# First mixer of a hybrid decoder step: the two heads of a pair in turns, the samples' inverse beside the last pair's, sample taps and channel sums on other engines, a fixed order at the end

## The chip, the cores and the metric

The kernel runs on one core of one Trainium2 chip. The metric is the device time of one execution in microseconds (us), the median of several runs. A core has five engines, each of which works off its own queue of instructions strictly in order: TensorE (PE in the rows; its weight loads are PEld), VectorE (DVE), ScalarE (ACT), GpSimd (POOL) and SyncE (SP), which here only issues DMAs. PE writes its products to banks of PSUM; the other engines take them from there.

## What is computed

One inference step of a two-layer trunk, on 512 new tokens of a prompt and on 8 samples of 4 tokens each, with the same weights. Layer 0 is the mixer that the change touches and a feed-forward block; layer 1 is a state-space mixer and a feed-forward block. The mixer, cut to what matters:

```python
def mixer_ab(x, conv_st, shift_st, wkv_st, w_in, conv_w, conv_b, ln_g, ln_b, mu, ...):
    p = x @ w_in                                   # 1024 -> 2816 channels
    pa, pb = p[..., :2 * D_A], p[..., 2 * D_A:]    # D_A = 512
    u = pa[..., :D_A] * jax.nn.sigmoid(pa[..., D_A:])
    ext = jnp.concatenate([conv_st, u], axis=1)
    ya = jax.nn.silu(layer_norm(causal_depthwise(ext, conv_w, conv_b), ln_g, ln_b))   # 31 taps
    q = pb + (prev - pb) * mu
    r, k, v, wl, al, gl = jnp.split(q, SPLIT_B, axis=-1)
    ...
    def step(s, inp):                              # 8 heads of 64, a 64 x 64 state each
        r_t, k_t, v_t, d_t, kk_t, a_t = inp
        sa = jnp.einsum('bhvk,bhk->bhv', s, -kk_t)
        s = s * d_t + sa[..., None] * (kk_t * a_t) + v_t[..., None] * k_t
        return s, jnp.einsum('bhvk,bhk->bhv', s, r_t)
    y, new_wkv = wkv_recurrence(r, k, v, decay, kk, a, wkv_st)
    y = group_norm(y) * lnx_g + lnx_b + bonus
    return jnp.concatenate([ya, y * g], axis=-1) @ w_out, ...
```

The layer norm of `ya` runs over the 512 channels. The recurrence is computed in chunks of 64 tokens, for which a triangular matrix per chunk and head has to be inverted.

## The kernel before

**Layout.** Channels lie on the 128 partitions, tokens along the free side: 544 tokens, 512 of the prompt and 32 of the samples, taken in two halves of 256 and 288. Weights come by DMA as 128 x 512 tiles (`wraw`); ACT makes a high part `whi` and DVE, for some POOL, a low part `wlo`. Inputs are split likewise (`xh`, `xl`). Every product with weights is three matmuls (`xh,whi`, `xl,whi`, `xh,wlo`), for each of 8 input tiles and two halves: 48 for an output tile of 128 channels. These are the matmuls of L201, called gemms here. The product with `w_in` has 22 output tiles. That with `w_out` has 8 output tiles, in two parts: part 0 takes the 4 tiles of channels of the convolution (24 gemms an output tile), the other part the 4 of the recurrence.

**The convolution.** For each of 4 channel tiles `conv_in` forms `u` (tiles `uext` for the prompt, `usam` for the samples) from its two gemm tiles. The 31 taps are each one DVE instruction on the prompt's sums (`cacc<-uext,cols,cacc`, 128 x 512) and one on the samples' (`cacc<-usam,cols,cacc`, 128 x 32). `conv_end` is the layer norm over all channels and comes when all four tiles have their taps: POOL adds up the four tiles, one matmul of a matrix of ones sums over partitions (L610), DVE subtracts the mean, ACT squares, POOL adds the squares, L622 sums them, then root, reciprocal, scaling and the split for `w_out`.

**The recurrence.** The 8 heads go as 4 pairs, numbered 0 to 3, one pair on 128 partitions. Of a pair:
- `pair_in` makes r, k, v, the decay and so on from the gemms.
- `pair_front` is `wkv_front` and `wkv_solve`. `wkv_front` issues 32 matmuls `ps_wf<-ar,kb` (L737, 64 rows, 128 columns): head 0 first, then head 1, the whole of a head through the one bank `wf` twice; DVE masks the result into `xa` and `xk`. DMAs bring the 16 x 16 diagonal blocks of `xa` through memory (`dx`, `xb`) to one block a partition; `wkv_solve` inverts them in 30 small POOL operations (`stmp`, `mm`); DMAs bring them back (`dm`, `mn`).
- `pair_mid` is `wkv_mid` and `wkv_tail`. It begins with the matmuls `ps_wo<-mn,xa` (L813, tile pz), which need `mn`; further products L821 to L843 complete the inverse, L852 multiplies it in, head 0 and then head 1, each in one bank of `wo`; L871 and L877 form what the scan needs.
- `pair_out` is `wkv_scan` (7 steps one behind the other: L894 on PE, then `st` on DVE), the matmuls L901 for the output, the norm of each head (L686, L706), the gate (L552) and the product `yb`.

The samples have their own path: `sample_front` (with an inverse of 16 blocks, L927 to L938), `sample_mid`, `sample_end`.

**What sets the order.** The stages are Python generators that `weave` advances by priorities while the gemms of `w_in` are emitted; a scheduler then orders each engine's queue. Banks of PSUM are taken by tag: 3 of `mm` for the gemms, 1 `wi`, 1 `wf`, 2 `wo`, 1 `wb`. The last calls of the mixer's first part are

```python
        weave((hi, pair_out(2)), (hi, pair_mid(3)), (md, sample_front()), (lo, conv_taps(3)))
        weave((hi, pair_out(3)), (hi, sample_out()), (0, conv_end()))
```

and the first part of `w_out` is emitted with the second of them.

## Time and profile before

| | |
|---|---|
| time, median of 3 runs | 1540.21 us (1530.88 to 1545.67) |
| the profiled execution | 1539.81 us |
| its span in the trace | 1538.0 us (1.8 us lie around it) |
| first mixer in the span | from 0 to about 441 us |
| PE, DVE, ACT, POOL busy | 1433.1, 1023.0, 603.9, 300.1 us |

The profiled execution lies 0.4 us under the median, so its rows can be read as those of a typical run. The three runs lie 14.8 us apart, about 1% of the time.

The change touches the first 441 us alone. The text speaks of four stages of it: 44 to 264 us, when the gemms of `w_in` run and everything else is woven between them; 264 to 338, from the last of these gemms to the first of `w_out`; 338 to 395, the first part of `w_out` with the last pair and the samples beside it; and 395 to 441, the second part of `w_out` and the norm behind it.

### The profile page before, as it was taken

Reading aid. Unit: us, or ns where it says so; the run is one execution under the profiler, and the core shown is the slowest. Engines: PE = TensorE matmul, PEld = TensorE weight load, DVE = VectorE, ACT = ScalarE, POOL = GpSimd, SP = SyncE. Lnnn points to the kernel's source line nnn. Section 1 sums busy time; section 2 is a strip of 40 time slices with the busy share of each in tenths; the row PEclk is TensorE's granted clock in tenths of the full one; section 3 lists DMA queues with packets and bytes.
Section 4 is the critical chain, followed back from the end, with each engine's and each line's share of the span. In section 5 each row is a group of like instructions: output and inputs, shape, how many; then the busy total and the mean of one; then the engine's idle time right before and its main releaser. Section 6 shows DMA issues by size and latency. Waiting matters only on the chain.

```text
span 1538.0 us, 30946 instructions
## 1 busy us (share of the span) xinstructions
PE 1433.1 (93%) x11952; PEld 1371.2 (89%) x11952; DVE 1023.0 (67%) x2437; ACT 603.9 (39%) x1385; POOL 300.1 (20%) x442
## 2 busy tenths in 40 slices
PE   7999999689879999999999879799989999999996
PEld 6987887468879999999999879799989999999996
DVE  6698796765888988656985557555575555554334
ACT  5444352141354445543222443243454444442222
POOL 1252542531320201001561311003200000000200
PEclk9999999689989999999999989789999999999998
DMA  5222113111214244423675469742212222222321
GB/s 187 73 61 66 45 53 102 21 26 50 83 40 130 87 143 171 153 90 111 201 209 180 163 211 306 229 136 89 81 61 91 88 85 90 90 83 86 93 76 59
DMA packets 131939, 169.13 MB, mean 110 GB/s; under 512 B 46912, under 2 KB 72512, under 8 KB 131536
## 3 DMA queue, kind: packets, MB, share of 16 engines
q1 hardware_dynamic: 107536, 130.47, 27.5%
q10 hardware_dynamic: 20944, 22.53, 4.5%
q0 software_dynamic: 3312, 14.16, 2.6%
q8 instruction: 94, 1.54, 0.4%
q14 instruction: 53, 0.43, 0.1%
HBM read 138.59 MB, written 32.71 MB: 111 GB/s over the span
## 4 chain that ended last, share of the span: by engine, by line
PE 73%; DVE 8%; DMA 7%; POOL 4%; issue 3%; ACT 3%; SPq 1%; ACTq 0%; POOLq 0%; DVEq 0%
PE ps_mm L201 62%; PE ps_wk L201 4%; POOL stmp L179 2%; POOL mm L179 2%; DVE wlo L179 2%; DVE xres L179 1%; DVE xres L176 1%; DMA wraw<-in_w_down 1%; PE ps_wf L737 1%; ACT xres L173 1%; DVE cacc L176 1%; DMA tm<-dt 1%; DMA du<-ue 1%; DMA dk<-s5a 1%; ACT whi L271 1%
## 5 line engine op out<-in xcount | busy, mean ns | idle before, releaser
L201 PE MATMUL ps_mm<-xh,whi 128*128 128x256 f32 (+1 forms) x2016 | 491.0, 298 | 19.4 <-ACT whi L271 6.5
L201 PE MATMUL ps_mm<-xl,whi 128*128 128x256 f32 (+1 forms) x2016 | 491.3, 295 | 5.2 <-DVE xl L176 5.0
L201 PE MATMUL ps_mm<-xh,wlo 128*128 128x256 f32 (+1 forms) x2016 | 490.2, 294 | 0.0
L179 DVE TENSOR_TENSOR wlo<-wraw,whi 128x512 fp32r<-128x512 f32 x342 | 255.4, 749 | 252.0 <-ACT whi L271 251.1
L271 ACT CAST whi<-wraw 128x512 fp32r<-128x512 f32 x372 | 226.1, 611 | 472.2 <-PE ps_mm L201 386.2
L201 PEld LDWEIGHTS ps_mm<-xh,whi 128*128 128x128 f32 x2016 | 354.3, 194 | 26.6 <-ACT whi L271 10.6
L201 PEld LDWEIGHTS ps_mm<-xl,whi 128*128 128x128 f32 x2016 | 356.3, 194 | 10.4 <-DVE xl L176 5.6
L201 PEld LDWEIGHTS ps_mm<-xh,wlo 128*128 128x128 f32 x2016 | 355.4, 193 | 4.3 <-issue 3.5
L201 PE MATMUL ps_mm<-fh,whi 128*128 128x256 f32 (+1 forms) x648 | 145.1, 290 | 0.0
L201 PE MATMUL ps_mm<-fl,whi 128*128 128x256 f32 (+1 forms) x648 | 144.5, 289 | 0.0
L201 PE MATMUL ps_mm<-fh,wlo 128*128 128x256 f32 (+1 forms) x648 | 144.3, 289 | 0.0
L201 PEld LDWEIGHTS ps_mm<-fh,whi 128*128 128x128 f32 x648 | 107.5, 188 | 1.8 <-issue 1.6
L201 PEld LDWEIGHTS ps_mm<-fh,wlo 128*128 128x128 f32 x648 | 107.7, 188 | 0.1
L201 PEld LDWEIGHTS ps_mm<-fl,whi 128*128 128x128 f32 x648 | 107.6, 188 | 0.0
L176 DVE SCALAR_TENSOR_TENSOR c<-ps_mm,cols,c 128x254 f32<-128x254 f32 (+3 forms) x264 | 98.5, 395 | 1.8 <-ACT edge L1195 1.4
L176 DVE SCALAR_TENSOR_TENSOR cacc<-uext,cols,cacc 128x512 f32<-128x512 f32 x120 | 94.3, 786 | 2.8 <-ACT cacc L173 1.5
L179 POOL TENSOR_TENSOR ln_s<-xres 128x256 f32<-128x256 f32 (+1 forms) x8 | 10.8, 1367 | 320.6 <-DVE xres L179 320.6
L179 POOL TENSOR_TENSOR wlo<-wraw,whi 128x512 fp32r<-128x512 f32 x30 | 39.6, 1332 | 150.5 <-ACT whi L271 146.5
L179 DVE TENSOR_TENSOR c<-ps_mm,c 128x256 f32<-128x256 f32 (+1 forms) x88 | 35.8, 437 | 49.2 <-PE ps_mm L201 47.1
L201 PE MATMUL ps_mm<-yl,whi 128*128 128x256 f32 (+1 forms) x240 | 57.7, 296 | 3.4 <-DVE yl L179 3.4
L201 PE MATMUL ps_mm<-yh,whi 128*128 128x256 f32 (+1 forms) x240 | 58.5, 299 | 0.3 <-ACT sg L173 0.3
L201 PE MATMUL ps_mm<-yh,wlo 128*128 128x256 f32 (+1 forms) x240 | 57.9, 296 | 0.0
(382 smaller groups left out, 2084.5 us busy)
## 6 DMA issues: line engine op xcount, KB each, us to landing
wraw<-in_w_up SPq DMA_DIRECT2D x176, 256.0 KB
wraw<-in_w_down SPq DMA_DIRECT2D x80, 256.0 KB
wraw<-in_w_in_ab SPq DMA_DIRECT2D x44, 256.0 KB
ds<-trig SPq DMA_DIRECT2D x8, 768.0 KB
ang<-ds POOLq DMA_DIRECT2D x8, 768.0 KB, 6.0
wraw<-in_w_out_c SPq DMA_DIRECT2D x21, 256.0 KB
wraw<-in_w_out_ab SPq DMA_DIRECT2D x16, 256.0 KB
df<-s5a ACTq DMA_DIRECT2D x8, 512.0 KB
```

What stands on the lines that cost most here:

```text
L173: return self.nc.scalar.activation(out, in_, f, **k)
L176: return self.nc.vector.scalar_tensor_tensor(out, a, s, b, op0, op1)
L179: return (eng or self.nc.vector).tensor_tensor(out, a, b, op=op)
L201: ins = self.nc.tensor.matmul(*a, **k)
L271: self.nc.scalar.copy(hi, src)
L737: nc.tensor.matmul(pa[:, i], lhsT=flat(kb[HS[hd], c // 2, c % 2]), rhs=ar[HS[hd], :, c], start=True, stop=True)
```

## The change

1. `wkv_front`: the two heads alternate, matmul by matmul, each with a bank of its own (`wf` and a bank of `wo`); the four DMAs to `dx` are issued at the end. In `wkv_mid` the matmuls of L852 (now L880) go to two banks, in the order of the blocks, which is four in a row on the same 64 x 64 quarter of PE.
2. The samples' 16 blocks are inverted in the same 30 POOL operations as the 64 of pair 3 (80 partitions); `sample_in` is woven into `pair_front(3)`.
3. The samples' taps: a POOL product of 128 x 496 (`spr<-usam,cols`, all 31 taps of two tokens of each sample, twice a channel tile), a DVE sum over taps, and the bias on ACT. The 120 DVE instructions of `cacc<-usam` go.
4. `conv_end`: four matmuls in a row into one bank sum over channels and partitions (L630, and L641 for the squares), in banks of `mm`; the sums on POOL go.
5. The order at the end: the matmuls L630 stand behind the last scan matmul of pair 2 (`scanned`); the first gemms of `w_out` (output tiles m = 0 and 1) follow; the first matmuls of `pair_mid(3)` (L840, before L813) stand behind the newest of these gemms (`behind`); the other output tiles are woven at low priority with `pair_mid(3)` and `pair_out(3)`.

The core of the diff:

```diff
@@ mm
-        ins = self.nc.tensor.matmul(*a, **k)
+        ins = self.newest = self.nc.tensor.matmul(*a, **k)
@@ conv_in, conv_taps
-            self.act(cs, usam[:, 0:32], AF.Identity, scale=w(0), bias=cb)
+            ws = self.cols[:, o:o + 31].unsqueeze(1).unsqueeze(1).broadcast_to([P, 2, NS, 31])
+            for j in range(0, NJ, 2):
+                pr = gp.tile([P, 512], F32, name="spr", tag="spr", bufs=1)
+                pr = pr[:, 0:2 * NS * 31].rearrange("p (j s t) -> p j s t", s=NS, t=31)
+                win = bass.AP(at.tensor, at.offset + NS * j, [at.ap[0], (NS, 2), (1, NS), (NS, 31)])
+                self.tt(pr, win, ws, ALU.mult, nc.gpsimd)
+                nc.vector.tensor_reduce(cs[:, NS * j:NS * j + 2 * NS].rearrange("p (j s) -> p j s", s=NS), pr,
+                                        mybir.AxisListType.X, ALU.add)
+            self.act(cs, cs, AF.Identity, bias=cb)
             for t in range(1, 31):
                 self.stt(ca, uext[:, t:t + NP], w(t), ca, ALU.mult, ALU.add)
-                self.stt(cs, usam[:, 8 * t:8 * t + 32], w(t), cs, ALU.mult, ALU.add)
@@ pair_front
+            solve = self.wkv_solve(p, [(dx, 8, self.mn), (dxs, 4, self.mns)])
+            for step in (front, front, sample, solve, front, solve, front, solve, front, sample, sample):
+                next(step)
+                yield
@@ conv_end
-                self.tt(s1[:, H], cacc[:, 0, H], cacc[:, 1, H], ALU.add, nc.gpsimd)
-                for i in (2, 3):
-                    self.tt(s1[:, H], s1[:, H], cacc[:, i, H], ALU.add, nc.gpsimd)
-                pm = self.bank([P, 512], "wf")
-                nc.tensor.matmul(pm[:, :n], lhsT=self.con("ones"), rhs=s1[:, H], start=True, stop=True)
+                pm = self.bank([P, 512])
+                for i in range(4):
+                    ins = nc.tensor.matmul(pm[:, :n], lhsT=self.con("ones"), rhs=cacc[:, i, H], start=i == 0, stop=i == 3)
+                    for b in behind:
+                        self.chain([b, ins])
                 for i in range(4):
                     self.stt(cacc[:, i, H], pm[:, :n], -1.0 / 512, cacc[:, i, H], ALU.mult, ALU.add)
-                    if i == 0:
-                        self.act(q[:, H], cacc[:, i, H], AF.Square)
-                    else:
-                        self.act(t[:, H], cacc[:, i, H], AF.Square)
-                        self.tt(q[:, H], q[:, H], t[:, H], ALU.add, nc.gpsimd)
+                    self.act(sqs[i][:, H], cacc[:, i, H], AF.Square)
@@ mixer_ab, the last calls
-        weave((hi, pair_out(2)), (hi, pair_mid(3)), (md, sample_front()), (lo, conv_taps(3)))
-        weave((hi, pair_out(3)), (hi, sample_out()), (0, conv_end()))
+        rest = conv_end(self.scanned)
+        weave((hi, pair_out(2)), (lo, conv_taps(3)), (lo, after(8, islice(rest, 6))))
+        behind = [self.newest]
+        weave((hi, seq(lambda: pair_mid(3, behind), lambda: pair_out(3))), (0, sample_out()), (lo, rest))
@@ wkv_front
-        for hd in range(2):
-            for g in range(2):
-                pa = self.bank([P, 4, 2, 64], "wf")
-                for i in range(4):
-                    c = 4 * g + i
+        for g in range(2):
+            pas = [self.bank([P, 4, 2, 64], t) for t in ("wf", "wo")]
+            for i in range(4):
+                c = 4 * g + i
+                for hd, pa in enumerate(pas):
                     nc.tensor.matmul(pa[:, i], lhsT=flat(kb[HS[hd], c // 2, c % 2]), rhs=ar[HS[hd], :, c], start=True,
                                      stop=True)
@@ wkv_mid
-        for h in range(2):
-            pw = self.bank([P, 4, 2, 64], "wo")
-            for c, c2, cp, j, hd, S, O in all_:
-                if hd == h:
-                    nc.tensor.matmul(pw[S, j].rearrange("p a t -> p (a t)"), lhsT=n64[S, h, cp],
+        pws = [self.bank([P, 4, 2, 64], "wo") for _ in range(2)]
+        for c, c2, cp, j, hd, S, O in all_:
+            nc.tensor.matmul(pws[hd][S, j].rearrange("p a t -> p (a t)"), lhsT=n64[S, hd, cp],
@@ wkv_scan
+            self.scanned[:] = [ins]
```

How the change moves instructions, at three places. On PE near the end of the gemms of `w_in`, the front of pair 3 before: groups of four of L737 into `wf` with gemms (L201) between them.

```order
L201 MATMUL ps_mm<-xl,whi 128x288
L201 MATMUL ps_mm<-xh,wlo 128x288
L737 MATMUL ps_wf<-ar,kb 128x128 x4
L201 MATMUL ps_mm<-xh,whi 128x288
L201 MATMUL ps_mm<-xl,whi 128x288
L201 MATMUL ps_mm<-xh,wlo 128x288
L894 MATMUL ps_wb<-st,gtt 64x64 x2
L528 MATMUL ps_wi<-xres,cons 128x256
L852 MATMUL ps_wo<-R,n_3076 64x128 x11
L737 MATMUL ps_wf<-ar,kb 128x128 x4
```

The same front after, on PE behind the last gemm of `w_in`; L851 and L858 are products of `pair_mid(2)` (before L821 and L828).

```order
L924 MATMUL ps_wb<-st,gtt 64x64 x4
L760 MATMUL ps_wf<-ar,kb 128x128
L760 MATMUL ps_wo<-ar,kb 128x128
L851 MATMUL ps_wo<-z,mn 32x32 x11
L760 MATMUL ps_wf<-ar,kb 128x128
L760 MATMUL ps_wo<-ar,kb 128x128
L760 MATMUL ps_wf<-ar,kb 128x128
L760 MATMUL ps_wo<-ar,kb 128x128
```

The heads alternate between two banks, and the front of pair 3 and most of `pair_mid(2)` no longer stand between gemms.

On PE at the turn to `w_out`, before: `conv_end` (L610, L622), the scan of pair 2 (L894) and `pair_mid(3)` (L843, L852) stand mixed.

```order
L843 MATMUL ps_wo<-n_3604,x 32x32 x14
L894 MATMUL ps_wb<-st,gtt 64x64
L901 MATMUL ps_wi<-qt,st 64x64 x2
L610 MATMUL ps_wf<-xres,cons 128x288
L852 MATMUL ps_wo<-R,n_3604 64x128
L894 MATMUL ps_wb<-st,gtt 64x64 x2
L901 MATMUL ps_wi<-qt,st 64x64 x2
L852 MATMUL ps_wo<-R,n_3604 64x128 x15
L622 MATMUL ps_wf<-xres,cons 128x256
```

There after (L924 is the scan, L969 and L970 the samples' front, L728 a head norm, L207 the gemms):

```order
L969 MATMUL ps_wf<-cons,sv 32x128
L970 MATMUL ps_wf<-cons,skb 64x128
L708 MATMUL ps_wi<-cons,sqt 128x2 x4
L924 MATMUL ps_wb<-st,gtt 64x64 x2
L976 MATMUL ps_wf<-swv,xs 32x64 x8
L924 MATMUL ps_wb<-st,gtt 64x64 x8
L630 MATMUL ps_mm<-cacc,cons 128x256 x4
L630 MATMUL ps_mm<-cacc,cons 128x288 x4
L728 MATMUL ps_wi<-cons,rq_y 64x128 x8
L641 MATMUL ps_mm<-xres,cons 128x256 x4
L641 MATMUL ps_mm<-xres,cons 128x288 x4
```

The scan of pair 2 ends ahead of `conv_end`, and nothing of pair 3 stands here any more: L840 follows 48 gemms of `w_out` further down.

On POOL, what stands ahead of the front of pair 3, before (`kb` is its input):

```order
L531 COPY sv<-v 128x32
L179 TENSOR_TENSOR sar<-xres,pexs 128x32
L179 TENSOR_TENSOR skb<-xres,rps 128x32
L179 TENSOR_TENSOR k<-k,xres 128x544
L179 TENSOR_TENSOR kb<-k,xres 128x4x64 x2
```

and after:

```order
L185 TENSOR_TENSOR sar<-xres,pexs 128x32
L185 TENSOR_TENSOR spr<-usam,cols 128x496
L185 TENSOR_TENSOR skb<-xres,rps 128x32
L185 TENSOR_TENSOR k<-k,xres 128x544
L185 TENSOR_TENSOR spr<-usam,cols 128x496
L185 TENSOR_TENSOR kb<-k,xres 128x4x64 x2
```

The two sample products of the last channel tile, which need the last gemm tile of `w_in`, now stand ahead of `kb` of pair 3.

## Rows read from the trace of the kernel before

**Rows 1.** Busy time by stage: window, length, busy of PE, PEld, DVE, ACT, POOL, PEclk, DMA share, GB/s.

```profile
44.00:264.00 220.00, 210.90 (x2130) 185.49 (x2130) 176.08 (x393) 86.20 (x189) 87.69 (x168) 0.96 0.24 66
264.00:338.00 74.00, 53.52 (x665) 40.34 (x664) 52.19 (x107) 23.23 (x55) 38.55 (x79) 0.74 0.14 30
338.00:395.00 57.00, 55.85 (x559) 46.20 (x560) 36.59 (x101) 12.12 (x32) 7.55 (x6) 0.89 0.16 53
```

**Rows 2.** PE's waits, 40 to 264 us: total, times, longest, in us.

```profile
PE ps_wo L813 <- DMA mn<-dm: 8.5, 4, 3.1
```

**Rows 3.** Timeline of DVE at the start: start, length, last column the wait before.

```profile
19.42 1.71 DVE L176 SCALAR_TENSOR_TENSOR cacc<-usam,cols,cacc 128x32 f32<-128x32 f32 x10
...
21.97 1.01 DVE L176 SCALAR_TENSOR_TENSOR wa<-ps_mm,cols,wa 128x256 f32<-128x256 f32 x3
```

**Rows 4.** Timeline of PE at the start.

```profile
22.50 0.56 PE L201 MATMUL ps_mm<-xh,whi 128*128 128x288 f32 x1 [2.42 <-DVE wa L176]
```

**Rows 5.** Timeline of PE around the last gemm of w_in.

```profile
261.79 1.16 PE L737 MATMUL ps_wf<-ar,kb 64*128 64x128 f32 x8
262.87 0.40 PE L201 MATMUL ps_mm<-xh,whi 128*128 128x288 f32 x1
...
263.24 0.29 PE L201 MATMUL ps_mm<-xh,wlo 128*128 128x288 f32 x1
...
264.36 1.52 PE L852 MATMUL ps_wo<-R,n 64*64 64x128 f32 x22
265.81 0.37 PE L737 MATMUL ps_wf<-ar,kb 64*128 64x128 f32 x1
```

**Rows 6.** PE's groups of instructions, 44 to 264 us.

```profile
L737 PE MATMUL ps_wf<-ar,kb 64*128 64x128 f32 x120 | 18.4, 288 | 0.0
```

**Rows 7.** Chain that ended last, 150 to 190 us: start, time on the chain.

```profile
155.43 0.95 PE ps_wf L756 x27
187.67 0.72 PE ps_wo L828 x18
```

**Rows 8.** Tile cacc, its taps: duration in ns min/median/max, first and last start.

```profile
L176 DVE SCALAR_TENSOR_TENSOR cacc<-usam,cols,cacc x120: 228/244/1353, 16.9 to 266.7; 128x32 f32<-128x32 f32 x120
L176 DVE SCALAR_TENSOR_TENSOR cacc<-uext,cols,cacc x120: 720/748/1819, 67.5 to 302.9; 128x512 f32<-128x512 f32 x120
```

**Rows 9.** Timeline of POOL, the inverse of pair 3.

```profile
276.68 0.67 POOL L179 TENSOR_TENSOR stmp<-xb,mm 64x15 f32<-64x15 f32 x1 [4.67 <-DMA xb<-dx]
...
294.40 0.21 POOL L179 TENSOR_TENSOR stmp<-xb,mm 64x15 f32<-64x15 f32 x1
```

**Rows 10.** Tile sm on POOL.

```profile
L179 POOL TENSOR_TENSOR sm<-swv,cons x2: 1488/1518/1549, 372.4 to 378.0; 128x512 f32<-128x512 f32 x2
```

**Rows 11.** Timeline of DVE, 264 to 338 us.

```profile
264.87 2.10 DVE L176 SCALAR_TENSOR_TENSOR cacc<-usam,cols,cacc 128x32 f32<-128x32 f32 x4
...
302.39 0.28 DVE L176 SCALAR_TENSOR_TENSOR st<-ps_wb,pend,xp 128x64 f32<-128x64 f32 x1 [6.36 <-PE ps_wb L894]
...
302.86 0.74 DVE L176 SCALAR_TENSOR_TENSOR cacc<-uext,cols,cacc 128x512 f32<-128x512 f32 x1
...
305.60 0.69 DVE L179 TENSOR_TENSOR z<-ps_wo,cons 128x512 f32<-128x512 f32 x1
```

**Rows 12.** Timeline of PE, 299 to 340 us.

```profile
301.44 0.58 PE L813 MATMUL ps_wo<-mn,xa 64*64 64x64 f32 x3 [6.91 <-DMA mn<-dm]
...
336.30 1.07 PE L877 MATMUL ps_wo<-xk,wv 128*64 128x64 f32 x16
337.83 0.58 PE L201 MATMUL ps_mm<-xh,whi 128*128 128x256 f32 x1 [0.46 <-ACT xh L271]
```

**Rows 13.** Matmuls of line 610: durations, first and last start.

```profile
L610 PE MATMUL ps_wf<-xres,cons x4: 379/444/483, 317.4 to 320.0; 128*128 128x256 f32 x2, 128*128 128x288 f32 x2
```

**Rows 14.** Chain that ended last, 264 to 445 us.

```profile
371.45 1.05 PE ps_wi L561 x2
...
394.74 6.73 PE ps_mm L201 x40
```

More of the change, by code (lines that the diff above doesn't have):

```diff
@@ L114, in constants, with seq @@
     return [np.concatenate([v[n] for n, _ in names], 1).astype(np.float32) for names in (_CONS, _CONS0)]
+def seq(*gens):
+    for g in gens:
+        yield from g()
 def after(n, gen):
@@ L812, in wkv_mid @@
         for c, c2, cp, j, hd, S, O in all_:
-            nc.tensor.matmul(pz[S, hd, cp], lhsT=xa[S, hd, c], rhs=mn[S, hd, cp, 0], start=True, stop=True)
+            ins = nc.tensor.matmul(pz[S, hd, cp], lhsT=xa[S, hd, c], rhs=mn[S, hd, cp, 0], start=True, stop=True)
+            for b in behind:
+                self.chain([b, ins])
         z = new("z", 64, "s2k", S2)
@@ L898, in wkv_scan @@
         py = self.bank([P, 8, 64], "wi")
[L899 removed]
+        for cs in ((1, 2), (3, 4), (5, 6), (7,)):
             for H in HS:
[L901 removed]
+                for c in cs:
+                    nc.tensor.matmul(py[H, c], lhsT=st[H, c], rhs=qt[H, c % 2, c // 2], start=True, stop=True)
         y = d["y"][:, 64:NP]
```

88 lines of the change are left out of this document (49 added, 39 removed).

## Prediction

> **What bounds the kernel now.** I read the busy time by stage first. While the gemms of `w_in` run (44 to 264 us), PE is busy 210.9 of 220 us at a granted clock of 0.96: PE is the bound, and what is taken from it there is gained [rows 1]. Its waits say what fills most of the rest: 8.5 us for `mn`, the inverse coming back by DMA [rows 2]. Between the last gemm of `w_in` and the first of `w_out` (264 to 338) PE is busy 53.5 of 74 us at 0.74: here it waits for others. DVE works through the taps of the last channel tile until 303.6, with a hole of 6.4 us, in which it waits for a scan matmul (L894) [rows 11]; PE at that time stands at the first matmul of `pair_mid(3)`, which waits 6.9 us for `mn` [rows 12]. Queues being in order, the scan of pair 2, DVE and so `conv_end` wait for the inverse of pair 3. L610 comes at 317.4 [rows 13], the first gemm of `w_out` at 337.8 [rows 12]. From 338 to 395 PE is full again, 55.9 of 57 us [rows 1], and the second part of `w_out` starts at 394.7 [rows 14]. That start is the landmark of my sum: behind it the program is the same, instruction for instruction, and bound by PE. The profiled execution took 1539.8, so a gain of g us at the landmark gives 1539.8 less g; it lies 0.4 under the median, which I neglect.
>
> **Start.** Before the first evacuation `wa`, DVE does at least ten sample taps in 1.7 us, and PE waits 2.4 us for it [rows 3, 4]. The taps go. I take 2.5 us off; between 0, if the input transfers set the pace, and 4, if the gemms after the wait come at a better clock.
>
> **Heads in turns.** Before, 8 matmuls L737 take from 261.79 to 262.87, 135 ns each [rows 5]. They use one half of PE's rows at a time. In turns, with a bank for each head, two can run at once. The nearest rows for overlapping small matmuls are L756 and L828, 64 columns, at 35 and 40 ns [rows 7]; for 128 columns L852 takes 1.45 us for 22, 66 ns [rows 5]. So the price halves, and for 96 matmuls of pairs 0 to 2 (120 stand in the window, 24 of them pair 3's [rows 6]) that is 96 x 0.069 = 6.6; I take 7 with pair 3's. Bounds: 0, if halves of rows do not overlap, and 7. The wait for `mn` should fall from 8.5 to about 6.5, since the front is shorter while DMAs and POOL's inverse stay; 2 us, give or take 4.
>
> The Trainium skill ("TensorEngine Tiling (Array Packing)", Gotcha 1) says that different row tiles cannot use the same PSUM bank at once, which would be the reason for 135 ns in one bank and bears out the halving. The same page (Key Properties) says that different tiles run in parallel, and so, read strictly, four L880 in a row on one tile would not; rows of L756 and L828, which are issued four in a row on a tile, stand at 35 and 40 ns against it.
>
> **What moves past the last gemm of `w_in`.** The 24 front matmuls of pair 3 in the window (3.2 us) and the products L821 to L843 of `pair_mid(2)` (128 at about 40 ns, 5.1 us), with single ones of L706 and L552: some 10 us that no longer stand between gemms but beside DVE's taps. The last gemm, at 263.2 [rows 5], so ends about 2.5 + 7 + 2 + 10 = 21.5 earlier, near 242.
>
> **From there to `conv_end`.** DVE sets this. Before it took from 264.9 to 303.6, 38.7 us. Less the hole (6.4, whose cause, pz of pair 3 in front of the scan, is moved away) and four sample taps (2.1 [rows 11]) it is 30.2. To it come evacuations of the front of pair 3 and of `pair_mid(2)` (about 6 us at 0.4 to 0.7 each), two sums over taps at the price of a 128 x 512 tile (0.69 [rows 11]), and a wait: POOL's two sample products now stand ahead of `kb`, at up to 1.5 us each [rows 10], so the front of pair 3 cannot start until some 8 us behind the last gemm, and DVE's evacuation of it stands between the taps: 2 to 4 us. Together 40; bounds 34 and 46. The scan of pair 2 now follows the taps, and L630 it. Nearest price: before, last tap 303.6 to L610 317.4, 13.8 us, in which five of the scan steps and the samples' front stood; I take 14, bounds 9 and 20. L630 is thus at 242 + 40 + 14 = 296, where L610 stood at 317.4.
>
> On POOL the first small operation of the inverse takes 0.67 us beside the taps and the same one 0.21 when DVE is done with most of them [rows 9]. The Trainium skill ("GPSIMD Engine Reference", Specifications) gives the reason, SBUF interfaces shared with VectorE where its instruction has two SBUF inputs; the trace agrees. By it the sample products, 8 of them, might cost DVE's taps too; their median of 748 ns [rows 8] already contains POOL's work, and I add nothing.
>
> **`conv_end`.** Before, L610 to the first gemm took 20.4 us. POOL's sums and their handoffs to ACT go (about 5), eight matmuls of sums more than before are added twice, at 0.4 each [rows 13], part of them beside the evacuations: 15, bounds 12 and 20. First gemm at 311 (before 337.8). 48 gemms for m = 0 and 1 at 0.13 to 0.17: 7.5. So the first matmul of `pair_mid(3)`, gated behind them, runs at 318.5, where it ran at 301.4. Its `mn` is there: the front ends near 265, before 266.9, and the inverse of 80 rows takes the same 30 operations.
>
> **The last pair.** Here the gain is given back. Before, from pz to the second part of `w_out` took 394.7 - 301.4 = 93.3 us: 36 to the end of L877 [rows 12], in part queued behind the samples' front and `conv_end`; then the scan between gemms, to L561 at 371.5; then the head norm and gate, 23.3 to 394.7 [rows 14]. Now `pair_mid(3)` has priority over the remaining 144 gemms, and its scan comes when they are gone, at 14 us or less, in place of 34. 36 less some 7 for what is no longer queued ahead, 14 and 23 make 73; gemms no longer between the norm's steps take 7 off: 66. PE's own work there, the 55.9 us of the stage [rows 1] less 7.5 for m = 0 and 1, lies below that. Landmark 318.5 + 66 = 384.5, 10.2 earlier: **1529.6**.
>
> **Rivals.**
> *The chain of pair 3 gives all back.* With 76 us in place of 66 the landmark is where it was: 1540. For it: scan and norms then run with PE empty and its clock low, which the 0.74 of the stage with waits shows [rows 1]. Against it: 93.3 contained the samples' front and `conv_end`.
> *Slower.* The gate puts pz behind `conv_end`, and everything of pair 3 behind pz. If that chain still takes what it took, 93.3, because each of its steps waits for the step before and not for a free engine, the landmark is 411.8, the time 1557. It decides from 76 us on.
> *Better.* If DVE takes 36 in place of 40 and the scan 10 in place of 14, and the tail takes 60, because the remaining gemms fill the gaps of `pair_mid(3)`, the gain is 10 + 4 + 4 + 6 = 24: 1516. For it: holes of 20 us in the second stage are what the fixed order fills. Against: DVE has little idle time there.
> *It does not do what it says.* If the halves of rows don't overlap, 7 are missing: 1537.
>
> If L880 does run alone on its tile, as the page's rule has it, it takes 135 in place of 66 ns, 128 x 0.069 = 8.8 us more, of which three quarters stand in stages bound by PE: 1536. I give this rival 3 in 100, as the rows speak against it.
>
> **How the numbers follow.** Forecast 0.40 (own range 1521 to 1538), all given back 0.19, slower 0.09, better 0.23, not as said 0.09 with L880. About 1% (15.4 us) is what a measurement of this kernel can tell from no change, since three runs of it lie that far apart. Faster by over 1% (below 1524.8): the better case, and a third of the forecast's, 0.36. Slower by over 1%: 0.08. Within: 0.56. The range leaves out the lower third of the better case and most of the slower one: 1508 to 1547.
>
> **What would show it.** Matmuls of the front in pairs at 60 to 70 ns, and no slower L880; DVE without `cacc<-usam`; the last gemm of `w_in` at 238 to 246; no hole in the taps before the scan; L630 near 296; first gemm near 311; L840 directly behind m = 1, without a wait for `mn`; the second part of `w_out` near 384. What would make it wrong: POOL's products slow enough (above 1.5 us) to hold the front in every pair; a scan of pair 2 of more than 20 us; the wait for `mn` growing with the POOL work; or a stage behind the mixer that starts at another clock.

## The result, and the profile after

The median is 1547.0 us over 20 runs (1535.0 to 1556.7), against 1538.5 for the kernel before (20 runs, 1524.6 to 1545.7): ratio 1.0067, 95% interval 1.0045 to 1.0088. The change makes the kernel 0.7% slower; 1529.6 was predicted, and the measured time lies at the upper edge of the range.

The profiled execution of the changed kernel took 1535.0 us, the lowest of its 20, so its span (1533.2 us) says nothing about the median: the unchanged program behind the landmark took 1129.6 us in it, 1143.3 in the profiled execution of before, and 1130.1 to 1150.5 in the traces of the experiments. What can be compared is the landmark itself, the start of the second part of `w_out`: 403.6 us, before 394.7 [rows 14], so 8.8 later. That the medians differ by as much is chance, since 13.7 us less lie behind it. Run 13 below, whose only edit is that SyncE issues four loads, shows an ordinary execution (1546.7 us of span): there the landmark is 412.3. Each landmark is that of one execution, so a few us between two of them show little by themselves.

Busy time by stage after, cut where the last gemm of `w_in`, the first of `w_out` and the landmark stand (columns as in [rows 1]):

```profile
44.00:247.00 203.00, 191.99 (x1923) 172.18 (x1922) 154.92 (x296) 82.53 (x183) 86.43 (x165) 0.95 0.23 61
247.00:320.00 73.00, 55.10 (x549) 40.60 (x547) 54.03 (x110) 20.86 (x46) 20.97 (x41) 0.72 0.21 54
320.00:404.00 84.00, 73.85 (x886) 61.58 (x887) 46.22 (x128) 18.91 (x51) 7.30 (x7) 0.79 0.11 37
404.00:450.00 46.00, 32.38 (x220) 31.76 (x219) 36.71 (x81) 16.49 (x35) 18.76 (x20) 0.83 0.26 85
```

The first stage is 17 us shorter and the second as long as before [rows 1]; the third takes 84 us in place of 57, at a granted clock of 0.79 in place of 0.89. The gain of the first stage is real and is spent in the third.

The timeline of PE after: last gemm of `w_in`; sums of `conv_end` (L630); first gemm of `w_out`; pz of pair 3; the head norm of pair 3; the landmark.

```profile
246.75 0.29 PE L207 MATMUL ps_mm<-xh,wlo 128*128 128x288 f32 x1
...
305.35 6.79 PE L630 MATMUL ps_mm<-cacc,cons 128*128 128x256 f32 x16
...
320.13 0.39 PE L207 MATMUL ps_mm<-xh,whi 128*128 128x256 f32 x1 [2.25 <-ACT xh L277]
...
332.70 0.68 PE L840 MATMUL ps_wo<-mn,xa 64*64 64x64 f32 x12
...
392.08 1.87 PE L708 MATMUL ps_wi<-cons,sqt 128*128 128x2 f32 x8 [1.36 <-ACT sqt L179]
...
397.90 1.98 PE L728 MATMUL ps_wi<-cons,rq_y 128*64 128x128 f32 x16 [0.46 <-DVE rq_y L182]
400.73 2.08 PE L581 MATMUL ps_wi<-gl,g 128*128 128x512 f32 x2 [0.85 <-DVE y L182]
403.58 0.82 PE L207 MATMUL ps_mm<-xh,whi 128*128 128x256 f32 x2 [0.78 <-DVE yb L185]
```

Against [rows 5, 12, 13]: 16.5 us earlier, 12.1 earlier (L610 then), 17.7 earlier, then pz 31.3 later and the landmark 8.8 later.

Where the second stage stays long is seen on DVE, POOL and PE. Timeline of DVE after: the last taps, the two halves of `xp` of pair 2, with which its `pair_mid` ends, and the first step of its scan.

```profile
277.93 8.62 DVE L182 SCALAR_TENSOR_TENSOR cacc<-uext,cols,cacc 128x512 f32<-128x512 f32 x11
288.48 0.42 DVE L185 TENSOR_TENSOR xp<-ps_wo,pend 128x256 f32<-128x256 f32 x1 [1.94 <-PE ps_wo L906]
...
295.06 0.42 DVE L185 TENSOR_TENSOR xp<-ps_wo,pend 128x256 f32<-128x256 f32 x1 [0.71 <-PE ps_wo L906]
...
297.49 0.28 DVE L182 SCALAR_TENSOR_TENSOR st<-ps_wb,pend,xp 128x64 f32<-128x64 f32 x1 [0.69 <-PE ps_wb L924]
```

Timeline of POOL in the same stretch: the first step of the merged inverse, a product for pair 3 (`yb`), the end of the inverse, and the copy that the scan of pair 2 begins with.

```profile
282.44 0.23 POOL L185 TENSOR_TENSOR stmp<-xb,mm 80x15 f32<-80x15 f32 x1 [24.56 <-DMA xb<-dxs]
...
287.68 1.33 POOL L185 TENSOR_TENSOR yb<-yb,v 128x544 f32<-128x544 f32 x1
...
296.35 0.61 POOL L824 COPY mm<-mm 80x256 f32<-80x256 f32 x1
296.82 0.23 POOL L920 COPY st<-xp 128x64 f32<-128x64 f32 x1
```

Timeline of PE, the first matmuls of that scan:

```profile
297.11 0.33 PE L924 MATMUL ps_wb<-st,gtt 64*64 64x64 f32 x4 [0.60 <-POOL st L920]
```

Before, the copy on POOL and the second half of `xp` on DVE:

```profile
287.25 0.77 POOL L890 COPY st<-xp 128x64 f32<-128x64 f32 x1
```

```profile
288.76 0.41 DVE L179 TENSOR_TENSOR xp<-ps_wo,pend 128x256 f32<-128x256 f32 x1
```

The taps end at 286.5, as forecast some 40 us behind the last gemm; but the scan starts 11 us later. It needs two things. One is the copy (`st<-xp`), which takes the first half of `xp` and stands right behind the whole inverse of pair 3 in POOL's queue; before, it stood inside the inverse and ran at 287.3. The other is the second half of `xp`, which the first step reads. `pair_mid(2)` has it at 295.5, before at 289.2, with taps still to do until 303.6. PE waits 0.60 us for the copy. So some 9 of the 11 us are the late `pair_mid(2)`, and at most 2 the copy.

Most products of `pair_mid(2)` ran between gemms before, and its second half of `xp` started 25.5 us behind the last gemm; now they run behind that gemm, beside the front of pair 3, and it is 48.3 us. PE's granted clock is 0.56 from 247 to 286 us, and it stands in the front of pair 3 for inputs from POOL and DVE; PE's waits, 248 to 440 us:

```profile
PE ps_wf L760 <- POOL kb L185: 4.6, 1, 4.6
PE ps_wf L760 <- DVE xk L185: 4.2, 1, 4.2
```

Since L630 is chained behind the scan, `conv_end` waits for it as well.

### The profile page after: what moved, and what is told of

It is laid out like the page before. It is cut to its first block, busy times and chain, and to the rows that moved or that the text cites. A ratio compares the mean times of both kernels' runs of the same rounds, so it can differ in the third digit from the quotient of the medians.

```text
span 1533.2 us, 30855 instructions
## 1 busy us (share of the span) xinstructions
PE 1424.0 (93%) x11976; PEld 1363.6 (89%) x11976; DVE 1003.5 (65%) x2325; ACT 604.1 (39%) x1385; POOL 281.2 (18%) x405
## 4 chain that ended last, share of the span: by engine, by line
PE 69%; DVE 12%; DMA 8%; ACT 3%; issue 3%; POOL 2%; SPq 1%; ACTq 0%; DVEq 0%; POOLq 0%
PE ps_mm L207 60%; DVE wlo L185 2%; DMA dy<-yg 2%; DVE cacc L182 1%; DVE xres L182 1%; DVE xres L185 1%; DMA ye<-dy 1%; DMA du<-ue 1%; PE ps_wk L207 1%; POOL mm L185 1%; DVE s5a L185 1%; ACT xres L179 1%; DMA wraw<-in_w_down 1%; POOL stmp L185 1%; DVE s5b L185 1%
## 5 line engine op out<-in xcount | busy, mean ns | idle before, releaser
L207 PE MATMUL ps_mm<-xh,whi 128*128 128x256 f32 (+1 forms) x2016 | 484.0, 296 | 21.8 <-DVE xres L185 6.5
L207 PE MATMUL ps_mm<-xl,whi 128*128 128x256 f32 (+1 forms) x2016 | 483.9, 293 | 4.0 <-DVE xl L182 3.9
L207 PE MATMUL ps_mm<-xh,wlo 128*128 128x256 f32 (+1 forms) x2016 | 484.7, 293 | 0.0
L185 DVE TENSOR_TENSOR wlo<-wraw,whi 128x512 fp32r<-128x512 f32 x342 | 250.6, 735 | 260.9 <-ACT whi L277 259.0
L207 PEld LDWEIGHTS ps_mm<-xh,whi 128*128 128x128 f32 x2016 | 350.9, 193 | 30.2 <-issue 10.4
L207 PEld LDWEIGHTS ps_mm<-xl,whi 128*128 128x128 f32 x2016 | 352.9, 192 | 7.0 <-DVE xl L182 4.6
L207 PEld LDWEIGHTS ps_mm<-xh,wlo 128*128 128x128 f32 x2016 | 351.7, 192 | 3.3 <-issue 2.2
L207 PE MATMUL ps_mm<-fh,whi 128*128 128x256 f32 (+1 forms) x648 | 145.1, 290 | 0.0
L207 PE MATMUL ps_mm<-fl,whi 128*128 128x256 f32 (+1 forms) x648 | 144.4, 289 | 0.0
L207 PE MATMUL ps_mm<-fh,wlo 128*128 128x256 f32 (+1 forms) x648 | 144.1, 288 | 0.0
L207 PEld LDWEIGHTS ps_mm<-fh,whi 128*128 128x128 f32 x648 | 107.3, 188 | 1.8 <-issue 1.6
L207 PEld LDWEIGHTS ps_mm<-fh,wlo 128*128 128x128 f32 x648 | 107.6, 188 | 0.1
L207 PEld LDWEIGHTS ps_mm<-fl,whi 128*128 128x128 f32 x648 | 107.6, 188 | 0.0
L182 DVE SCALAR_TENSOR_TENSOR c<-ps_mm,cols,c 128x255 f32<-128x255 f32 (+3 forms) x264 | 98.1, 393 | 0.9 <-ACT edge L1227 0.6
L207 PE MATMUL ps_mm<-yh,whi 128*128 128x256 f32 (+1 forms) x240 | 58.8, 299 | 7.9 <-ACT yh L277 7.6
L207 PE MATMUL ps_mm<-yl,whi 128*128 128x256 f32 (+1 forms) x240 | 57.7, 295 | 0.0
L207 PE MATMUL ps_mm<-yh,wlo 128*128 128x256 f32 (+1 forms) x240 | 57.6, 294 | 0.0
```

Source lines behind the costliest of these rows:

```text
L182: return self.nc.vector.scalar_tensor_tensor(out, a, s, b, op0, op1)
L185: return (eng or self.nc.vector).tensor_tensor(out, a, b, op=op)
L207: ins = self.newest = self.nc.tensor.matmul(*a, **k)
```

## The experiments

Every run is compared with the kernel before on the same chip. The median of before lies between 1533.9 and 1538.5 us on these chips, so two runs are compared by their ratios here; 0.1% is 1.5 us. The landmark is that of the run's profiled execution. The changed kernel has one more edit, which the list of its parts leaves out: the output matmuls of the scan (L933) go two chunks of a head at a time. Runs 1, 2, 3, 5, 13, 14, 15 and 17 have it, the others don't, and none tries it alone.

| run | kernel | median us | ratio to before | interval | landmark |
|---|---|---|---|---|---|
| | before | 1538.5 | | | 394.7 |
| | changed, parts 1 to 5 | 1547.0 | 1.0067 | 1.0045 to 1.0088 | 403.6 |
| 1 | changed, no gate | 1554.6 | 1.0123 | 1.0077 to 1.0168 | 417.7 |
| 5 | changed, no chain behind the scan | 1537.5 | 1.0016 | 0.9988 to 1.0044 | 396.7 |
| 17 | changed, neither | 1536.0 | 1.0001 | 0.9976 to 1.0026 | 396.5 |
| 2 | parts 1 to 4, order of before | 1529.9 | 0.9945 | 0.9919 to 0.9971 | 390.9 |
| 7 | before and part 5 | 1549.5 | 1.0098 | 1.0065 to 1.0130 | 413.5 |
| 4 | before and part 1 | 1525.8 | 0.9934 | 0.9910 to 0.9958 | 388.6 |
| 8 | the same, held in turn | 1537.3 | 1.0030 | 1.0003 to 1.0056 | 397.4 |
| 6 | before and part 3 | 1523.5 | 0.9930 | 0.9897 to 0.9963 | 380.1 |
| 10 | before and part 4 | 1532.9 | 0.9974 | 0.9944 to 1.0004 | 390.0 |
| 11 | before and part 2 | 1529.3 | 0.9969 | 0.9941 to 0.9997 | 388.0 |
| 9 | parts 1, 3 | 1541.9 | 1.0046 | 1.0017 to 1.0074 | 396.4 |
| 12 | parts 1, 2, 3 | 1538.7 | 1.0020 | 0.9991 to 1.0048 | 396.6 |
| 16 | parts 2, 3, 4 | 1525.9 | 0.9947 | 0.9924 to 0.9970 | 384.8 |
| 18 | parts 1, 3 but for the last tile | 1532.4 | 0.9976 | 0.9945 to 1.0006 | 399.2 |
| 3 | changed, part 3 undone | 1539.1 | 1.0026 | 0.9997 to 1.0055 | 399.5 |
| 13 | changed, loads by SyncE | 1547.8 | 1.0081 | 1.0058 to 1.0104 | 412.3 |
| 14 | changed, `spr` behind `kb` | 1554.6 | 1.0136 | 1.0109 to 1.0163 | 412.8 |
| 15 | changed, part 2 undone | 1552.9 | 1.0117 | 1.0088 to 1.0146 | 410.5 |

### The fixed order (runs 1, 2, 7, 5, 17)

The theory was that part 5 spends what parts 1 to 4 gain, by holding pair 3 behind the gate (the chain from the gemms of m = 1 to pz); the rival, that the stretch behind the last gemm is held by other engines whatever the order.

Run 1:

```diff
-        weave((hi, seq(lambda: pair_mid(3, behind), lambda: pair_out(3))), ...
+        weave((hi, seq(lambda: pair_mid(3), lambda: pair_out(3))), ...
```

> The changed kernel without the gate: pair_mid(3) no longer stands behind the gemms of m = 1, everything else as changed; the scheduler puts its first matmuls (L840) back into the scan of pair 2, ahead of conv_end. Theory G (the gate and the fixed order hold pair 3 back: L840 ran at 332.8 us of the trace where it ran at 301.4 before): L840 near 302, where the inverse of pair 3 comes back; the second part of w_out starts at 380 to 392 in place of 403.6, and the time falls by 12 to 24 us against the changed kernel, to 1523 to 1535. Rival D (the stretch after the last gemm of w_in is held by VectorE, by the late front of pair 3 and by a slow TensorE, not by the gate): L840 in the scan brings its wait for mn back in front of DVE's scan steps, the second part starts at 398 to 406, and the time is that of the changed kernel within 5 us.

Measured: 1.2% slower than before; against the changed kernel the intervals still touch. pz ran at 303.5, as the theory had it, but between the first two steps of the scan of pair 2 (300.9 and 315.1), whose last matmul came at 326.4, and L630 behind that at 326.9. The theory falls as stated: while `conv_end` waits for the scan, the gate protects the scan.

Run 2:

```diff
-        rest = conv_end(self.scanned)
-        weave((hi, pair_out(2)), (lo, conv_taps(3)), (lo, after(8, islice(rest, 6))))
-        behind = [self.newest]
-        weave((hi, seq(lambda: pair_mid(3, behind), lambda: pair_out(3))), (0, sample_out()), (lo, rest))
+        weave((hi, pair_out(2)), (hi, pair_mid(3)), (lo, conv_taps(3)))
+        weave((hi, pair_out(3)), (hi, sample_out()), (0, conv_end([])))
```

> The changed kernel with the last calls as before (pair_mid(3) woven with pair_out(2), conv_end with pair_out(3), no gate, conv_end free of the scan), parts 1 to 4 kept. Theory G: parts 1 to 4 are a gain of their own, as the last gemm of w_in 16 us earlier shows, and the order spends it: second part of w_out at 375 to 388, time 1518 to 1531, as good as without the gate or better. Rival D: parts 1 to 4 move work behind the last gemm and give no more than they take: second part at 393 to 402, time 1537 to 1546.

Measured: 1529.9, 1.2% under the changed kernel and 0.55% under before. Parts 1 to 4 are a gain, and part 5 costs some 19 us. The first gemm of `w_out` is no earlier for it (319.2), but pz runs at 308.6, beside `conv_end`, and the landmark comes 12.7 us earlier.

Run 7 is the reverse: the kernel before with the lines that run 2 takes out, the gate in `wkv_mid` and the chain at `conv_end`.

> The kernel before with part 5 alone: conv_end behind the scan of pair 2, the gemms of m = 0 and 1 behind it, pair_mid(3) gated behind them, the rest woven with pair_mid(3) and pair_out(3); the samples' front woven with pair_out(2). Theory O (the order costs by itself some 15 us, whatever else is changed): second part of w_out at 404 to 414, time 1548 to 1558. Rival (the order costs only because parts 1 to 4 bring the front of pair 3 and the scan of pair 2 behind the last gemm): second part at 392 to 399, time 1534 to 1543.

Measured: 1.0% slower, landmark 413.5. The order costs 15 us without the other parts, too.

Run 5:

```diff
-        rest = conv_end(self.scanned)
+        rest = conv_end([])
```

> The changed kernel without the chain from the last scan matmul of pair 2 to the sums of conv_end (L630); the gate on pair_mid(3) stays. Theory S (of the fixed order, the scan in front of conv_end is what costs, since conv_end then waits for two chains one behind the other): the sums start when the taps are done, first gemm of w_out at 308 to 314 in place of 320, second part at 390 to 397 in place of 403.6, time 1533 to 1540. Rival P (the gate on pair_mid(3) is what costs): the time stays within 4 us of the changed kernel's 1547, the second part within 3 us of 403.6.

Measured: 0.5% (some 8 us) under the changed kernel, landmark 396.7; time and landmark lie inside theory S. The sums start with the taps' end; the timeline of PE in run 5, the first of the sums and the first gemm of `w_out`:

```profile
287.52 1.18 PE L630 MATMUL ps_mm<-cacc,cons 128*128 128x256 f32 x4
...
313.51 0.38 PE L207 MATMUL ps_mm<-xh,whi 128*128 128x256 f32 x1
```

L630 18 us earlier than in the changed kernel, and the first gemm 6.6.

Run 17 makes both edits, of runs 1 and 5.

> The changed kernel with neither chain: conv_end free of the scan of pair 2 and pair_mid(3) free of the gemms of m = 1; the last calls stay woven as changed. It completes the square: both chains 1547, without the gate alone 1555, without the scan's chain alone 1538. Theory S (the scan in front of conv_end is what costs, and the gate only bites because conv_end stands in front of it): 1530 to 1538, second part of w_out at 388 to 396, like the order of before with the same parts (1530). Rival P (the shape of the last calls costs too: pair_mid(3) and pair_out(3) one behind the other, gemms at low priority): 1538 to 1548.

Measured: 1536.0. The square, as ratios to before: both chains 1.0067, no gate 1.0123, no scan chain 1.0016, neither 1.0001. The scan's chain costs 0.5% (8 us) with the gate and 1.2% (19 us) without it; the gate costs nothing measurable by itself. What is left to run 2, 0.56% (some 9 us), goes with the shape of the last calls, which no run takes apart.

In the seven traces of kernels with the gate the landmark comes 70.9 to 72.5 us behind pz. So with the gate, what holds up pz holds up the landmark by as much.

### The parts alone (runs 4, 8, 6, 10, 11)

Run 4 applies the hunks of `wkv_front` and `wkv_mid` to the kernel before.

> The kernel before with part 1 alone: heads in turns with a bank each in wkv_front, L852 in the order of the blocks. Theory G and the prediction: 128 matmuls of the front at 65 to 70 ns in place of 135, the last gemm of w_in 6 to 8 us earlier (255 to 257), the second part of w_out 3 to 8 earlier, time 1530 to 1536. Rival (halves of rows give nothing, or the front waits for a second bank of wo as long as it gains): last gemm at 262 to 264, time as before, 1538.

Measured: 0.66% faster, more than forecast, and not by the price per matmul. Timeline of PE after, a front of pair 0, its first half in pairs and the other half alone, and L880:

```profile
61.94 0.27 PE L760 MATMUL ps_wf<-ar,kb 64*128 64x128 f32 x1
61.95 0.27 PE L760 MATMUL ps_wo<-ar,kb 64*128 64x128 f32 x1
62.05 0.27 PE L760 MATMUL ps_wf<-ar,kb 64*128 64x128 f32 x1
...
66.62 1.16 PE L760 MATMUL ps_wf<-ar,kb 64*128 64x128 f32 x8
...
149.26 2.01 PE L880 MATMUL ps_wo<-R,n 64*64 64x128 f32 x32
```

Two in turn take 0.11 us, 55 ns each where [rows 5] had 135. But only 16 of 32 go so: the second half goes out as 8 of one head and 8 of the other, at 135 ns. That saves 16 x 0.08 = 1.3 us a front, 4 us over three fronts. In run 4 the wait for `mn` fell; PE's waits, 40 to 264 us:

```profile
PE ps_wo L816 <- DMA mn<-dm: 1.7, 2, 1.2
```

It was 8.5 [rows 2]. But other waits took its place, for `kb`, `R`, `xk` and others: PE's waits up to the last gemm are 10.5 us in all, before 9.1. The last gemm is 14 us earlier (248.9) mostly because work has moved behind it: from 44 us to it PE is busy 194 us in place of 210, and the price accounts for 4 of the 16.

Run 8 holds all 32 in turn:

```diff
+                    if prev is not None:
+                        self.chain([prev, ins])
+                    prev = ins
```

> The kernel before with part 1 alone and the 32 matmuls of a front held in the order in which they are written, so that all stand in pairs of one head each (heads alone issues half of them as 8 of one head and then 8 of the other). Theory H (pairs run at 55 ns each, single ones at 135): 16 x 0.08 = 1.3 us a front less than heads alone, last gemm 2 to 4 us earlier than its 248.9, time 1519 to 1524. Rival (a pair needs two free banks at once, and PE stands in its queue for the second): a new wait of the front for xa or xk, time 1526 to 1534.

Measured: 1.0% slower than run 4, beyond the rival's range. PE's waits in run 8, 40 to 247 us:

```profile
PE ps_wo L820 <- DMA mn<-dm: 8.0, 3, 4.9
PE ps_mm L201 <- DVE v L176: 2.6, 1, 2.6
```

The wait for `mn` is back, and yet the last gemm comes at 245.0, 3.9 us earlier than in run 4, as theory H has it. The loss stands behind it: the first gemm of `w_out` comes 14.4 us later than in run 4 (339.9), and in between the front waits 4.3 us for `xk`, as the rival has it. The profiled execution is the slowest of its 12, so these times are rough. The gain of part 1 is thus not that of pairs at 55 ns alone; that it hangs on where the scheduler can put the front is argued, not shown.

Run 6 applies the hunk of `conv_taps` to the kernel before.

> The kernel before with part 3 alone: the samples' taps as POOL products and sums over taps. From the samples' taps put back (8 us faster than the changed kernel): theory K (the products stand ahead of kb on POOL, so that every front is late) time 1541 to 1548, the last gemm of w_in 2 to 6 us later than 263. Rival (they cost only together with the fixed order at the end, where the front of pair 3 is late): last gemm 258 to 263, time 1532 to 1539, the start 2 us earlier.

Measured: 0.7% faster, below both ranges; with run 4 the fastest of all, and the intervals don't separate the two. Timeline of POOL in run 6, and the second half of `xp` on DVE:

```profile
243.73 1.43 POOL L179 TENSOR_TENSOR kb<-k,xres 128x256 f32<-128x256 f32 x2
245.11 0.26 POOL L179 TENSOR_TENSOR skb<-k,rps 128x32 f32<-128x32 f32 x1
255.29 1.97 POOL L179 TENSOR_TENSOR spr<-usam,cols 128x496 f32<-128x496 f32 x1 [9.92 <-DVE usam L179]
...
269.46 0.23 POOL L179 TENSOR_TENSOR stmp<-xb,mm 64x15 f32<-64x15 f32 x1 [3.54 <-DMA xb<-dx]
...
270.87 0.24 POOL L899 COPY st<-xp 128x64 f32<-128x64 f32 x1 [0.38 <-DVE xp L179]
```

```profile
274.68 0.41 DVE L179 TENSOR_TENSOR xp<-ps_wo,pend 128x256 f32<-128x256 f32 x1
```

Here the products stand behind `kb`, the front of pair 3 starts at 246.0 ahead of the last gemm (254.4), the copy comes at 270.9, at the head of the inverse, and `pair_mid(2)` ends with `xp` at 274.7: the scan's last step is at 288.6, before the taps are done.

Run 10 (hunk of `conv_end`) and run 11 (hunk of `pair_front`, with the `wkv_solve` of the change):

> The kernel before with part 4 alone: 16 matmuls of ones for the sums over channels and 16 for the squares, in banks of mm, in place of POOL's additions and 8 matmuls. Prediction: POOL's sums and their handoffs to ACT go, conv_end some 5 us shorter, second part of w_out at 388 to 392, time 1531 to 1536. Rival C (fp32 matmuls at 0.4 us each, 0.42 at the low clock, take 6 us where POOL worked beside the rest): conv_end as long as before or longer, second part at 394 to 400, time 1537 to 1544.

> The kernel before with part 2 alone: the samples' 16 blocks inverted with pair 3's 64, sample_in woven into the front of pair 3. Prediction: 30 POOL operations and their DMA chain less, nothing on the path: time within 3 us of the kernel before, second part at 391 to 396. Rival D (the inverse of pair 3 now waits for the samples' blocks, which come from later matmuls, and pz of pair 3 for both): pz at 304 to 312 in place of 301.4, second part at 398 to 404, time 1541 to 1548.

Measured: 0.26% faster, which may be nothing, and 0.3% faster. The landmarks (390.0, 388.0) are inside and below the range of the prediction; rivals C and D fall, though pz of run 11 came at 305.2, as rival D has it.

### The parts together (runs 9, 12, 16, 18, 3)

Run 9 has the edits of runs 4 and 6.

> The kernel before with parts 1 and 3 (heads in turns, samples' taps on POOL), which alone took 0.7% each. Theory A (their gains add: one takes small matmuls and the wait for mn off TensorE, the other instructions off VectorE): second part of w_out at 372 to 378, time 1510 to 1518 against 1534 to 1538 of the kernel before. Rival B (they take the same wait, since with either the stretch behind the last gemm is held by the front of pair 3): second part at 379 to 389, time 1521 to 1528.

Measured: neither; 0.46% slower than before, where the gains would have made it 1.4% faster. Timeline of POOL in run 9, and the second half of `xp` on DVE:

```profile
256.43 1.50 POOL L179 TENSOR_TENSOR spr<-usam,cols 128x496 f32<-128x496 f32 x1 [0.94 <-DVE rq_y L702]
257.89 1.86 POOL L179 TENSOR_TENSOR kb<-k,xres 128x256 f32<-128x256 f32 x2
...
300.36 0.60 POOL L806 COPY mm<-mm 64x256 f32<-64x256 f32 x1
...
303.79 0.23 POOL L901 COPY st<-xp 128x64 f32<-128x64 f32 x1
```

```profile
303.88 0.42 DVE L179 TENSOR_TENSOR xp<-ps_wo,pend 128x256 f32<-128x256 f32 x1
```

The same instructions as in run 6, in another order: the products ahead of `kb`, the front at 259.1, and the copy behind the inverse, at 303.8. `pair_mid(2)` is no earlier: its second half of `xp` comes at 303.9, 29 us later than in run 6.

Run 12 adds part 2.

> The kernel before with parts 1, 2 and 3; with part 4 it is the changed kernel under the order of before, which took 0.55% off. If the merged inverse costs (rival D of the run with part 2 alone): 6 to 12 us slower than parts 1 and 3, and as fast as with part 4. If the sums cost (rival C of the run with part 4 alone): as fast as parts 1 and 3, 6 to 12 us faster than with part 4.

Measured: as fast as run 9 within the intervals, so the merged inverse does not cost; with part 4 and the new order of L933 in addition (run 2) it is 0.75% faster.

Run 16 has parts 2, 3 and 4.

> The kernel before with parts 2, 3 and 4, without heads in turns and without the fixed order: each of the three alone was as fast as before or faster. Theory I (what is lost in sums of parts is lost between heads in turns and the taps on GpSimd, since the front of pair 3 then stands behind the products; without the heads the parts add): second part of w_out at 370 to 378, time 1512 to 1521. Rival (any two parts move the scheduler's order as much as heads and taps did): second part at 385 to 397, time 1528 to 1542.

Measured: 1525.9, between the two; no better than part 3 alone.

Run 18 keeps the last tile's taps on DVE:

```diff
-            for j in range(0, NJ, 2):
+            for j in range(0, NJ if i < 3 else 0, 2):
...
+                if i == 3:
+                    self.stt(cs, usam[:, 8 * t:8 * t + 32], w(t), cs, ALU.mult, ALU.add)
```

> The kernel before with heads in turns and the samples' taps on GpSimd for three of the four channel tiles; those of the last stay on VectorE, so that nothing that needs the last gemm of w_in stands in front of kb of pair 3. Theory K (heads and taps do not add because the last two products hold the front of pair 3, 259 in place of 249): front of pair 3 at 248 to 252, second part of w_out at 376 to 386, time 1514 to 1526. Rival (the scheduler's order differs in many places and no single one holds it): front late or not, time 1530 to 1543.

Measured: 1532.4, within the rival; the front still started at 256.1, and PE waited 5.4 us for `kb` even so. Part of what run 9 lost comes back (0.7%), not the sum.

Run 3 puts all samples' taps of the changed kernel back on DVE.

> The changed kernel with the samples' taps on VectorE again, 120 instructions of 128 x 32 (part 3 undone). Theory G: the front of pair 3 starts 4 to 5 us earlier (no products ahead of kb on POOL), DVE does 8 us more of taps behind the last gemm and 3 at the start; the second part of w_out moves by -2 to +4 us against 403.6. Rival D, in the form that POOL's products are the trouble: the second part 6 to 10 us earlier, time 1537 to 1541.

Measured: 1539.1, 0.4% (some 6 us) faster than changed, as the rival has it, but the intervals touch; the landmark, 399.5, is 4 us earlier. What gains 0.7% alone gains nothing here, and may cost 0.4%.

### The stretch before the scan (runs 13, 14, 15)

Run 13, in `sample_end`:

```diff
-            nc.scalar.dma_start(out=s0[p], in_=self.I["wkv"][:, p])
+            nc.sync.dma_start(out=s0[p], in_=self.I["wkv"][:, p])
```

> The changed kernel with the four loads of the samples' state (s, L1018) issued by SyncE instead of ScalarE. In the trace of the changed kernel the last tap ends at 286.5 us, but the scan of pair 2 begins at 297, and in between ScalarE stands 4 us at the issue of one of these loads, which waits for yb on GpSimd, queued behind the first steps of the merged inverse. Theory M (this chain, merged inverse, yb, load, ScalarE's copies, holds the scan and so conv_end): the scan begins 3 to 6 us earlier, L630 at 299 to 302 in place of 305.3, second part of w_out 3 to 6 earlier, time 1541 to 1544. Rival N (TensorE's own queue of small matmuls at the low clock holds it): L630 within 1.5 us of 305.3, time 1545 to 1549.

Measured: no change. ScalarE no longer stands there, and the second half of `xp` comes 45.8 us behind the last gemm in place of 48.3 (298.0 in that execution). But now PE waits 3.2 us for the copy, right behind the inverse (302.3, inverse done at 302.4). Theory M falls in the form with ScalarE.

Run 14 chains `spr` of the last tile behind `kb` of pair 3 on POOL.

> The changed kernel with the sample products of the last channel tile held behind kb of pair 3 on GpSimd, as they stand when part 3 is made alone. Theory K (the products in front of kb, 12 us between sar and kb, delay the front of pair 3 and with it everything to the gate): the front starts at 250 to 252 in place of 256.1, the inverse and the scan 3 to 5 us earlier, second part at 398 to 401, time 1541 to 1544. Rival (the merged inverse waits for the samples' blocks and not for the front of pair 3): inverse at 282, L630 and the time within 2 us of the changed kernel.

Measured: 0.7% slower than changed. `kb` was early, but the front came at 255.3, hardly earlier (256.1), since PE then stood 2.7 us at DVE's `rq_y` and, further on, 6.2 at `xk`, and the scan's end moved to 314.7. Theory K falls.

Run 15 goes back to two inverses.

> The changed kernel with part 2 undone: pair 3's 64 blocks inverted as soon as they are there, the samples' 16 in a run of their own behind them, the samples' front woven with pair_out(2); fixed order kept. Theory M (the merged inverse waits 24 us for the samples' blocks on an empty GpSimd and holds yb back): inverse of pair 3 at 276 to 278 in place of 282.4, scan of pair 2 and L630 4 to 8 us earlier, second part at 396 to 400, time 1538 to 1543. Rival (part 2 is harmless, as alone, where it took 0.3% off): L630 and time within 2 us of the changed kernel, or later by the second run of 30 operations.

Measured: 0.5% slower than changed; the intervals touch. The inverse of pair 3 started at 278.7 and ended at 295.7, yet the copy came at 298.5 and the first scan step at 303.3; the scan then ended at 312.7. Shortening what stands ahead of the copy did not bring the scan forward, for the second half of `xp` came behind the copy. Timeline of DVE in run 15:

```profile
301.58 0.42 DVE L185 TENSOR_TENSOR xp<-ps_wo,pend 128x256 f32<-128x256 f32 x1
...
303.32 0.28 DVE L182 SCALAR_TENSOR_TENSOR st<-ps_wb,pend,xp 128x64 f32<-128x64 f32 x1
```

## Why the prediction was wrong

The sign was wrong because part 5, put down as a gain, costs 1.0 to 1.2% (runs 2 and 7). In the sum that is the term for the stretch from the last tap to L630, and what follows from it. Step by step, predicted and as in the profiled execution of the changed kernel:

- **Last gemm of `w_in`:** 242; 246.8 (252.1 in run 13). The start gave what was said: the wait for `wa` ended 1.1 us earlier (21.4), and the granted clock from there to 44 us was 1.00, before 0.92. The 7 us for heads in turns were mis-sized: 4 by the matmuls, for half of them go alone. Nor can a bank shared by two halves be the reason for the 135 ns of the eight L737, which are of one head, on one half. The wait for `mn` fell to 3.6 us (6.5 forecast), but others took its place: PE's waits up to the last gemm are 10.7 us in all, before 9.1.
- **Taps:** 40 us, measured 39.8, in part by luck, as single items were off: `spr` took 1.98 us in the median, above my bound of 1.5.
- **Last tap to L630 (the step that failed):** 14 us; measured 18.9, and in kind otherwise than I took it: 11 until the scan starts and 8 for the scan. I priced it by the stretch before, in which, as I wrote, five of the scan steps stood. Before, the scan ran beside the taps: DVE has three of its seven steps ahead of the last tap's end (303.6), one between that and L610 (317.4), and three behind L610. The fourth and fifth:

```profile
306.28 0.28 DVE L176 SCALAR_TENSOR_TENSOR st<-ps_wb,pend,xp 128x64 f32<-128x64 f32 x1
...
317.65 0.28 DVE L176 SCALAR_TENSOR_TENSOR st<-ps_wb,pend,xp 128x64 f32<-128x64 f32 x1
```

I let DVE's taps alone set the stretch and took the scan as ready when they end. But I had moved the products of `pair_mid(2)`, which the scan needs, behind the last gemm, and counted only their evacuations on DVE; they were done 9 us behind the last tap. Then I chained `conv_end` behind this scan. Runs 5 and 17 show that the chain costs: 0.5% with the gate, 1.2% without. That the scan is late because `pair_mid(2)` is late is read from the traces (its second half of `xp` at 274.7 in run 6, 288.8 before, 295.1 changed, 303.9 in run 9); no run moves these products alone, and none moves the copy to another engine, which held PE for 0.6 us here and 3.2 in run 13.

- **`conv_end`:** 15; 14.8. Right in sum; L630 took 6.8 us, 0.42 for each of its 16 records.
- **m = 0 and 1:** 7.5; 12.6. A wait of 1.5 us for `yb`, the output matmuls of the scan (L933) and a head sum stood between them, and the granted clock was 0.74 from 320 to 333 us.
- **Last pair:** 66; 70.9. The sum has a slip: 36 less 7, 14 and 23 make 66 and not 73, so that with the last 7 taken off too it is 59 and the forecast 1522.6. What was mis-sized is `pair_mid(3)`, 36 less 7, which took 41.9 from pz to the end of L906: PE was busy 41.5 us of it at a granted clock of 0.98, 20.7 of them with the remaining 144 gemms, which stood between its steps, as did products of the samples. Pair 3's scan and norm run when the gemms are gone, as I said: the scan took 13.8 of the 14 us, norm and gate 15.2 of the 16 (23 less 7), although the granted clock was 0.50, the lower level of 1.2 GHz, from 388 us on: L708, L728 and L581 took 1.87, 1.98 and 2.08 us.

The terms add up to some 19 us, from a gain of 10.2 to a loss of 8.8. That the time behind the landmark would be that of before was wrong too, by 13.7 us in this execution. My rival for the slower side had the right place (all of pair 3 behind `conv_end`) and the wrong mechanism: the chain from pz took 70.9, not 93.3; it was pz that came late, 332.7 for 318.5. The gate, which I took for the risk, costs nothing measurable without the scan's chain (runs 5 and 17).

L880, four in a row on one tile, took 61 ns each (32 in 1.94 us), L852 before 66 [rows 5]. The Trainium skill ("TensorEngine Tiling (Array Packing)", Key Properties) says that different tiles can run in parallel; read strictly, the four on one tile would go one by one. At the 135 ns of L737 they would then take longer than they did, so the measurement speaks against that reading; what one L880 takes alone was not measured.

Settled: parts 1 to 4 with the order of before gain 0.55%; part 5 costs 1 to 1.2% with or without them. In the changed kernel 0.5% of that is the chain behind the scan; with both chains gone, 0.56% is left, which goes with the shape of the last calls. Open: what in that shape costs, and why the parts don't add. Runs 9 and 6 hold the same products and copies in other places of POOL's queue, and run 18 shows that the two products ahead of `kb` are only a part of it. The best kernels here are runs 6 and 4, part 3 or part 1 alone, 0.7% under before; their intervals overlap, with each other and with that of run 2.
